# First layer's head of a hybrid decoder trunk: x in channel halves on a second queue, first weights in idle buffers, a written order for three engines

## The chip, the core and the metric

The kernel runs on one core of one Trainium2 chip. The metric is the device time of one execution in microseconds, the median of several runs; lower is better. Engines are called PE (TensorE), DVE (VectorE), ACT (ScalarE), POOL (GpSimd) and SP (SyncE, which only issues transfers here).

## What is computed

Two pre-norm decoder layers over 256 tokens with 1024 channels, batch 1. What matters here is the start of a layer:

```
h    = rms_norm(x, ln1_gain[l])            # over the 1024 channels
proj = h @ w_in[l]                         # 1024 -> several groups of columns
cos, sin = rope tables of positions        # three head groups use them
```

Columns of `proj` feed sparse attention (six heads), latent attention (five heads, low-rank queries and keys) and retention (five heads); their outputs go through `w_out`, and then comes a squared-ReLU MLP with `w_up` (1024 to 4096) and `w_down`. Everything is float32; the large products are made in three (or two) passes on a high and a low part of each operand.

## The kernel before

The 256 tokens are two tiles `t` of 128 rows. `xs` holds x with tokens on partitions; `xT` holds it transposed, channels on partitions, as a pair (high part, low part). Eight blocks `kt` of 128 channels make up the contraction.

**High and low parts.** `split` (L140 and L141) makes the pair: an ACT copy rounds the operand to the format of the fast product (`hi`), and a second engine, DVE unless told otherwise, subtracts it from the operand (`lo`). `mm3` (L146 to L148) makes three products of a pair with a pair. So each weight tile costs a transfer, an ACT copy, a DVE subtraction and then products on PE.

**The stream of weights.** `Stream` holds all weight tiles ("units") in the order of use. `get` loads up to LOAD_AHEAD units ahead and splits up to SPLIT_AHEAD ahead. Raw tiles come from a pool of five (`raw_tile`), split pairs from another pool of five (`hilo`); a transfer into a raw tile waits until the split that read it last is done. All transfers of units are issued by SP in the order of the list, one after the other. Eight semaphores go round among the transfers of the hardware queues, so a transfer also waits for the one eight places before it.

**The head.** Columns of `w_in` come in chunks: A (434 columns: gates and the latent vectors, four units of two channel blocks each, `raw_A`), then B2, B1, B3 (384 columns, four units each, `raw_B`), then rq, rk, rg, rv. For layer 0 the head loads constants `c0s` (identity matrix, frequencies), x and the gain, transposes x on PE (L486), multiplies by the gain on DVE (L493, `xg`), splits that into `xT`, and starts chunk A's products (48 of 128x434, `l_A`). Both tiles' halves are done by `norm_half`, four times. `rope_tables` computes sines and cosines of the positions: a chain of DVE operations on 128x96 values (`rt`), two sines on ACT, copies into `tab_c` and `tab_s`. `sum_sq` (L505) makes the sums of squares, from which the scale `rstd` follows; it is applied when a chunk leaves PSUM (L563). Eight products on zeros (`ps_idle`, L176) run on PE while nothing has landed. Two of chunk A's four low parts are made on POOL (START_POOL).

**The order** of the instructions on each engine comes from a scheduler in the tile framework that works with priorities (`PRIO`) and its own estimate of times; `issue_after` sets one instruction behind another. After chunk A the latent attention's small products (`ps_cT`, `ps_uq`, `ps_uk`, `ps_uv`) are mixed with B2 and B1. The compression weights (`raw_w`, eight transfers of 256 KB in rows of 512 bytes) come between B1 and B3 in the stream; their products are `ps_h`.

Of the kernel before, what the change touches and what calls it, by code (L numbers as in the profile page):

```python
# [48 lines left out]
START_POOL = (1, 2)  # L49
# [28 lines left out]
def tile_hybrid_trunk(  # L78
# [65 lines left out]
    def mm3(o, a, b, start, stop):  # L144

        nc.tensor.matmul(o, a[1], b[0], start=start, stop=False)  # L146
        nc.tensor.matmul(o, a[0], b[1], start=False, stop=False)  # L147
        nc.tensor.matmul(o, a[0], b[0], start=False, stop=stop)  # L148
# [16 lines left out]

    g8 = p2.tile([8, P], F32, name="g8", tag="h_sb", bufs=1)
    nc.sync.dma_start(c0s, c0)
    nc.sync.dma_start(xs[:, 0, 0:512], xv[:, 0, 0:512])
    nc.sync.dma_start(g8, ln1_gain[0].rearrange("(k p) -> k p", p=P))
    nc.sync.dma_start(xs[:, 0, 512:D], xv[:, 0, 512:D])  # L170
# [4 lines left out]
    for _ in range(WARM):  # L175
        nc.tensor.matmul(ps_idle[:, 0:P], idle, idle, start=True, stop=True)  # L176

    def late_start():
        nc.sync.dma_start(xs[:, 1, :], xv[:, 1, :])

    nc.gpsimd.dma_start(pos_i, positions.rearrange("o (t p) -> p (o t)", p=P))
# [18 lines left out]
    def rope_tables():  # L200
# [3 lines left out]
        nc.vector.tensor_copy(pos_f, pos_i)  # L204
# [3 lines left out]
        for t in range(2):  # L208
            nc.vector.tensor_scalar(ang[:, t], c0s[:, C_INV:C_INV + nf], pos_f[:, t:t + 1], None, op0=ALU.mult)

        def rounded(o, src, period):
            nc.vector.tensor_scalar(o, src, 1.0 / period, MAGIC, op0=ALU.mult, op1=ALU.add)
            nc.vector.tensor_scalar(o, o, MAGIC, None, op0=ALU.subtract)

        def less(o, k, part, src):
            nc.vector.scalar_tensor_tensor(o, in0=k, scalar=-part, in1=src, op0=ALU.mult, op1=ALU.add)
# [7 lines left out]
        nc.vector.tensor_scalar(u, k2, -small[2], None, op0=ALU.mult)  # L224
        less(u, k1, big[2], u)
        nc.vector.tensor_tensor(r, r, u, op=ALU.add)
        nc.vector.tensor_scalar(r, r, PI_LO, -PI_LO, op0=ALU.min, op1=ALU.max)
        nc.scalar.activation(s1, r, AF.Sin)
        nc.scalar.activation(s2, r, AF.Sin, scale=0.5)
        nc.vector.tensor_tensor(u, s2, s2, op=ALU.mult)  # L230
        nc.vector.tensor_scalar(u, u, -2.0, 1.0, op0=ALU.mult, op1=ALU.add)
        for off, sl, n in ((0, slice(0, 16, 2), 8), (16, slice(0, 16), 16), (48, slice(16, 48), 32)):
# [958 lines left out]
```

## Time and profile before

| | |
|---|---|
| time of three runs | 667.03, 668.58, 671.0 us; median 668.58 us |
| time of the profiled execution | 666.31 us |
| its span, first to last instruction | 664.5 us |
| PE busy | 641.7 us, 97% of the span |
| DVE, ACT, POOL busy | 456.0, 380.4, 75.6 us |
| mean granted TensorE clock | 0.991 of full speed |

The profile shows one execution. Its own time is 1.8 us over its span (start and end of the program), and 2.3 us below the median of the three runs. A row of a timeline gives start, duration, engine, line, operation, destination and sources; in brackets stand the engine's idle time ahead of it and what ended that. Consecutive instructions overlap a little, so a step costs less than its duration. SPq is SP issuing a transfer.

### The profile page before, as it was taken

The numbers are of one execution on the slowest core, as the hardware profiler recorded it, in microseconds if no ns is written. First come the engines' busy times: TensorE is split into PE (matmuls) and PEld (weight loads), VectorE is DVE, ScalarE is ACT, GpSimd is POOL, SyncE is SP. The second block draws the span as 40 slices with busy tenths as digits, with TensorE's granted clock in tenths as the row PEclk, the third lists the DMA queues.
The fourth block names the chain that finished last, engine by engine and source line by source line (L and its number), as shares of the span: only waits on it lengthen the run. The fifth ranks groups of instructions, "written<-read, shape, count | busy, mean of one in ns | idle before, by whom it ended". The sixth has DMA issues, their size and how long they took to land.

```text
span 664.5 us, 10416 instructions
## 1 busy us (share of the span) xinstructions
PE 641.7 (97%) x3619; PEld 549.9 (83%) x3619; DVE 456.0 (69%) x1059; ACT 380.4 (57%) x895; POOL 75.6 (11%) x128
## 2 busy tenths in 40 slices
PE   7998999999999999999999999999799999999995
PEld 6998997677888888888889999867588888888884
DVE  6756878767866666666676597877686666666663
ACT  5968776555554545454486787736384444444442
POOL 3520500210000000000033051130100000000000
PEclk7999999999999999999999999999999999999998
DMA  7897554043756565656548665423075665656521
GB/s 238 268 173 245 169 184 111 33 128 127 251 177 212 166 214 167 217 165 206 150 143 175 199 191 155 110 86 127 20 265 167 214 203 177 202 178 200 181 64 63
DMA packets 79797, 111.64 MB, mean 168 GB/s; under 512 B 9721, under 2 KB 67969, under 8 KB 79617
## 3 DMA queue, kind: packets, MB, share of 16 engines
q1 hardware_dynamic: 79136, 108.89, 54.0%
q0 software_dynamic: 608, 2.10, 0.9%
q8 instruction: 28, 0.46, 0.3%
q14 instruction: 25, 0.20, 0.1%
HBM read 109.92 MB, written 1.05 MB: 167 GB/s over the span
## 4 chain that ended last, share of the span: by engine, by line
PE 88%; DVE 5%; DMA 4%; ACT 2%; issue 1%; POOL 0%; POOLq 0%; SPq 0%; ACTq 0%; DVEq 0%
PE ps_up L1032 18%; PE ps_up L1033 9%; PE l_pd L146 9%; PE l_pd L148 9%; PE l_pd L147 9%; PE l_po L146 2%; PE l_po L148 2%; PE l_po L147 2%; DMA raw_rq<-in_w_in_dram 2%; PE l_oT L864 2%; PE l_B L146 1%; PE l_B L147 1%; PE l_B L148 1%; PE ps_pT L872 1%; PE ps_s L811 1%; DMA raw_B<-in_w_in_dram 1%
## 5 line engine op out<-in xcount | busy, mean ns | idle before, releaser
L1032 PE MATMUL ps_up<-xT,hi_wu 128*128 128x512 f32 x512 | 178.5, 393 | 0.5 <-DVE u_s L1044 0.5
L1033 PE MATMUL ps_up<-xT,lo_wu 128*128 128x256 f32 x512 | 140.6, 280 | 0.0
L141 DVE TENSOR_TENSOR lo_wd<-raw_wd,hi_wd 128x1024 fp32r<-128x1024 f32 x64 | 78.2, 1225 | 55.8 <-ACT hi_wd L140 55.4
L1032 PEld LDWEIGHTS ps_up<-xT,hi_wu 128*128 128x128 f32 x512 | 95.7, 188 | 22.0 <-DVE u_s L1044 1.1
L148 PE MATMUL l_pd<-hi_wd,u_h 128*128 128x512 f32 x256 | 100.6, 393 | 0.0
L146 PE MATMUL l_pd<-hi_wd,u_l 128*128 128x512 f32 x256 | 100.5, 394 | 0.0
L147 PE MATMUL l_pd<-lo_wd,u_h 128*128 128x512 f32 x256 | 99.7, 390 | 0.0
L1033 PEld LDWEIGHTS ps_up<-xT,lo_wu 128*128 128x128 f32 x512 | 96.0, 188 | 2.1
L140 ACT CAST hi_wu<-raw_wu 128x512 fp32r<-128x512 f32 x128 | 72.5, 618 | 35.3 <-issue 27.0
L141 DVE TENSOR_TENSOR lo_wu<-raw_wu,hi_wu 128x512 fp32r<-128x512 f32 x128 | 82.2, 686 | 14.5 <-ACT hi_wu L140 14.4
L140 ACT CAST hi_wd<-raw_wd 128x1024 fp32r<-128x1024 f32 x64 | 67.0, 1050 | 36.4 <-PE l_pd L148 22.3
L148 PEld LDWEIGHTS l_pd<-hi_wd,u_h 128*128 128x128 f32 x256 | 48.1, 188 | 11.2
L146 PEld LDWEIGHTS l_pd<-hi_wd,u_l 128*128 128x128 f32 x256 | 48.1, 188 | 10.2
L147 PEld LDWEIGHTS l_pd<-lo_wd,u_h 128*128 128x128 f32 x256 | 48.1, 188 | 9.6
L140 ACT CAST u_h<-u_u 128x512 fp32r<-128x512 f32 x32 | 19.8, 620 | 53.1 <-DVE u_u L1046 52.8
L1043 ACT COPY u_s<-ps_up 128x256 f32<-128x256 f32 x64 | 23.3, 368 | 36.8 <-PE ps_up L1033 36.8
L141 DVE TENSOR_TENSOR lo_B<-raw_B,hi_B 128x192 fp32r<-128x192 f32 (+1 forms) x80 | 28.6, 414 | 21.8 <-ACT hi_B L140 21.7
L1044 DVE TENSOR_TENSOR u_s<-ps_up,u_s 128x256 f32<-128x256 f32 x64 | 26.7, 421 | 23.0 <-ACT u_s L1043 23.0
L141 DVE TENSOR_TENSOR u_l<-u_u,u_h 128x512 fp32r<-128x512 f32 x32 | 22.1, 691 | 17.9 <-ACT u_h L140 17.9
L828 ACT ACTIVATE p_nsa<-p_nsa,nsa_m 128x256 f32<-128x256 f32 (+2 forms) x72 | 28.6, 400 | 8.0 <-DVE nsa_m L826 7.8
L147 PE MATMUL l_B<-lo_B,xT 128*128 128x384 f32 x96 | 32.9, 342 | 0.0
L140 ACT CAST hi_B<-raw_B 128x192 fp32r<-128x192 f32 (+1 forms) x80 | 25.1, 381 | 13.5 <-DMA raw_B<-in_w_in_dram 6.7
(320 smaller groups left out, 1246.1 us busy)
## 6 DMA issues: line engine op xcount, KB each, us to landing
raw_wu<-in_w_up_dram SPq DMA_DIRECT2D x64, 512.0 KB, 4.5
raw_wd<-in_w_down_dram SPq DMA_DIRECT2D x64, 512.0 KB, 4.2
raw_B<-in_w_in_dram SPq DMA_DIRECT2D x24, 384.0 KB, 3.8
raw_wo<-in_w_out_dram SPq DMA_DIRECT2D x10, 512.0 KB, 4.1
raw_A<-in_w_in_dram SPq DMA_DIRECT2D x8, 434.0 KB, 4.5
raw_wo<-in_w_out_dram SPq DMA_DIRECT2D x12, 256.0 KB, 4.2
raw_w<-in_cmp_w_k_dram SPq DMA_DIRECT2D x8, 256.0 KB, 6.1
raw_w<-in_cmp_w_v_dram SPq DMA_DIRECT2D x8, 256.0 KB, 5.7
```

What stands on the lines that cost most here:

```text
L140: a = nc.scalar.copy(out=hi, in_=src)
L141: b = eng.tensor_tensor(lo, src, hi.bitcast(F32), op=ALU.subtract)
L146: nc.tensor.matmul(o, a[1], b[0], start=start, stop=False)
L147: nc.tensor.matmul(o, a[0], b[1], start=False, stop=False)
L148: nc.tensor.matmul(o, a[0], b[0], start=False, stop=stop)
L811: nc.tensor.matmul(o, qT[g][:, r, t * P:(t + 1) * P], kT[i][:, g, a:b], start=i == 1, stop=i == 0)
L828: nc.scalar.activation(p[:, o:o + n], p[:, o:o + n], AF.Exp, scale=-1.0, bias=ms[:, r, b:b + 1], accum_out=ls[:, r, b:b + 1])
L864: nc.tensor.matmul(oT[gp, 0:384], kv_sb[kt][:, vi, gp], pTs[g][:, 0:384], start=i == 0, stop=False)
L1032: nc.tensor.matmul(ps[j], w[0][:, o:o + P], x2, start=i == 0 and k == 0, stop=False)
L1033: nc.tensor.matmul(ps[j][:, 0:S], w[1][:, o:o + P], x2[:, 0:S], start=False, stop=i == 1 and k == 3)
L1043: nc.scalar.copy(sj, ps[j][:, S:512])
L1044: nc.vector.tensor_tensor(sj, ps[j][:, 0:S], sj, op=ALU.add)
```

## The change

- x comes in four pieces (tile t, half h of the channels), issued by ACT on its own queue. First come the two first halves, with the gain between them. SP's queue starts with the constants, then the positions (before: issued by POOL), then chunk A's four units.
- Chunk A's raw weights go into the memory of `mixT`, which the mixers fill later. The five raw tiles are thereby free for B2's first unit, `uq`, `uk` and two more units of B2.
- A class `Line` sets each instruction of the head behind the one before it on the same engine: `vec` for DVE, `act_` for ACT, `ten` for PE. On DVE the whole first part of the rope tables comes first, then the gain, the splits of the first halves of x and of the first two units of A, then the rest of the tables. On ACT all sines come first. POOL makes no split any more.
- PE transposes the first halves of both tiles, makes another eight products on zeros (WARM_ON), then unit 0 of chunk A for both tiles; the second halves of x are transposed behind that.
- Splits of A come in pieces of 434 columns instead of 868. Chunk A accumulates in two other banks of PSUM (`att` in place of `acc`).
- The sines go straight to their tables with scale 1 or -1 (six ACT operations in place of one and six DVE copies); the cosine's last step writes the table.
- Small transfers of the mixers (`l_nrm`, `l_w2s`) move from SP to POOL, and the order of units puts B2's first unit ahead of the latent attention's.

```diff
-START_POOL = (1, 2)
+WARM_ON = 8
...
+    def x_part(t, h):
+        nc.scalar.dma_start(xs[:, t, h * 512:(h + 1) * 512], xv[:, t, h * 512:(h + 1) * 512])
...
     nc.sync.dma_start(c0s, c0)
-    nc.sync.dma_start(xs[:, 0, 0:512], xv[:, 0, 0:512])
-    nc.sync.dma_start(g8, ln1_gain[0].rearrange("(k p) -> k p", p=P))
-    nc.sync.dma_start(xs[:, 0, 512:D], xv[:, 0, 512:D])
+    x_part(0, 0)
+    nc.sync.dma_start(pos_i, positions.rearrange("o (t p) -> p (o t)", p=P))
+    nc.scalar.dma_start(g8, ln1_gain[0].rearrange("(k p) -> k p", p=P))
+    x_part(1, 0)
...
-    nc.gpsimd.dma_start(pos_i, positions.rearrange("o (t p) -> p (o t)", p=P))
...
-        nc.scalar.activation(s1, r, AF.Sin)
-        nc.scalar.activation(s2, r, AF.Sin, scale=0.5)
...
+        act_(lambda: nc.scalar.activation(s2, r, AF.Sin, scale=0.5))
+        groups = ((0, slice(0, 16, 2), 8), (16, slice(0, 16), 16), (48, slice(16, 48), 32))
+        for off, sl, n in groups:
             for half in range(2):
...
+                act_(lambda: nc.scalar.activation(tab_s[:, :, off + half * n:off + (half + 1) * n], r[:, :, sl], AF.Sin,
+                                                  scale=1.0 if half else -1.0))
...
         def load():
-            raw = raw_tile(name)
+            if home:
+                if home not in homes:
+                    homes[home] = p1.tile([P, 2, 1024], F32, name="raw_" + home, tag=home)
+                raw = homes[home][:, part]
+            else:
+                raw = raw_tile(name)
...
-                     nc.gpsimd if (l, name) == (0, "A") and i in START_POOL else nc.vector)
+                     home=f"mixT{i // 2}" if (l, name) == (0, "A") else None, part=i % 2)
...
+        add_chunk(l, "A")
+        add_chunk(l, "B2", 1)
         add_mla(l)
-        add_chunk(l, "B2")
+        add_chunk(l, "B2", 3, 1)
         add_cmp(l)
+        add_chunk(l, "B2", 4, 3)
...
+    class Line:
...
+        def __call__(self, f):
+            with tc.issue_after(self.last.ins) if self.last else nullcontext():
+                self.last = f()
...
+    def start_parts(hi, lo, src):
+        act_(lambda: nc.scalar.copy(out=hi, in_=src))
+        vec(lambda: nc.vector.tensor_tensor(lo, src, hi.bitcast(F32), op=ALU.subtract))
+        return act_.last, vec.last
...
-    for u in W.units[:W.index["x1"] + 1]:
+    for u in W.units[:4]:
         u[2] = u[0]()
         W.loaded += 1
+    x_part(0, 1)
+    x_part(1, 1)
...
+            W.hold((0, "B2", 0))
+            rope_finish = rope_tables(vec, act_)
+            ps = [start_transposes(0, 0)]
...
+            act_(lambda: sum_sq(0, 0, ss1))
+            ps.append(start_transposes(1, 0))
+            ten(lambda: warm(WARM_ON))
+            xg = [start_gain(t, 0, ps[t]) for t in range(2)]
+            start_x(0, 0, xg[0])
+            start_w(0, 0)
+            start_x(1, 0, xg[1])
+            start_w(0, 1)
+            start_w(1, 0)
+            start_w(1, 1)
+            rope_finish()
+            act_(lambda: sum_sq(1, 0, ss1))
...
+        def start_rest(ss1=ss1):
+
+            ps = [start_transposes(t, 1) for t in range(2)]
+            xg = [start_gain(t, 1, ps[t]) for t in range(2)]
+            for t in range(2):
+                start_x(t, 1, xg[t])
+            for i in (2, 3):
+                for j in range(2):
+                    start_w(i, j)
+            for t in range(2):
+                act_(lambda: sum_sq(t, 1, ss1))
+            factors()
+            W.load_to(LOAD_AHEAD)
+            W.release((act_.last, vec.last), SPLIT_AHEAD)
+            W.hold((0, "B2", 1))
```

The order of instructions that results, at two places. First ACT at the start of the program. Before (a DMA that an engine issues stands in its order too; `hi_A` and `raw_A` are the units of chunk A, `junk` is the sum of squares, `rt` the rope chain):

```order
L140 ACT_TABLE_LOAD
L140 CAST hi_A_202<-raw_A_103 128x868
L140 CAST xT<-xg 128x4x128 x2
L140 CAST hi_A_206<-raw_A_200 128x868
L140 CAST hi_A_212<-raw_A_210 128x868
L140 CAST xT<-xg 128x4x128
L140 CAST hi_A_218<-raw_A_216 128x868
L140 CAST xT<-xg 128x4x128
L505 ACTIVATE junk,l_ss_106<-xs 128x512 x4
```

and now (`raw_mixT` is chunk A's raw weights in their new place):

```order
L167 DMA xs<-in_x_dram 128x512 x3
L234 ACT_TABLE_LOAD
L234 ACTIVATE rt<-rt 128x96
L238 ACTIVATE tab_s<-rt 128x2x8 x2
L238 ACTIVATE tab_s<-rt 128x2x16 x2
L238 ACTIVATE tab_s<-rt 128x2x32 x2
L557 ACTIVATE junk,l_ss_111<-xs 128x512
L539 CAST xT<-xg 128x4x128
L539 CAST hi_A_168<-raw_mixT_103 128x434
L539 CAST xT<-xg 128x4x128
L539 CAST hi_A_168<-raw_mixT_103 128x434
L539 CAST hi_A_176<-raw_mixT_103 128x434 x2
```

Seven sines and one sum of squares now stand ahead of the first copy into `xT`. On DVE, likewise, all 16 operations of the rope chain (L209 to L233, the last of which writes the argument of the sines) stand ahead of the gain `gT`, which stood behind the seventh before.

Second, SP's transfers behind chunk A, up to the compression weights. Before (`l_pos_t` are 16 transfers of 8 KB, `c1s` the masks, 1056 KB):

```order
L371 DMA raw_uq_225<-in_mla_w_uq_dram 128x2x480
L402 DMA l_w2s<-in_cmp_w_k_dram 128x64
L404 DMA l_pos_t<-in_cmp_pos_k_dram 16x2x64 x2
L379 DMA raw_uk_227<-in_mla_w_ukv_dram 128x5x64 x2
L404 DMA l_pos_t<-in_cmp_pos_k_dram 16x2x64 x4
L323 DMA raw_B_0_230<-in_w_in_dram 128x2x384
L404 DMA l_pos_t<-in_cmp_pos_k_dram 16x2x64 x2
L323 DMA raw_B_1_232<-in_w_in_dram 128x2x384
L323 DMA raw_B_2_234<-in_w_in_dram 128x2x384
```

and now:

```order
L349 DMA raw_B_0_247<-in_w_in_dram 128x2x384
L397 DMA raw_uq_252<-in_mla_w_uq_dram 128x2x480
L405 DMA raw_uk_254<-in_mla_w_ukv_dram 128x5x64 x2
L349 DMA raw_B_1_257<-in_w_in_dram 128x2x384
L349 DMA raw_B_2_259<-in_w_in_dram 128x2x384
L430 DMA l_pos_t<-in_cmp_pos_k_dram 16x2x64 x8
L430 DMA l_pos_t<-in_cmp_pos_v_dram 16x2x64 x8
L480 DMA c1s<-c_dram 128x2113
L151 DMA l_gng<-in_ret_gn_gain_dram 128x320
L349 DMA raw_B_3_282<-in_w_in_dram 128x2x384
L349 DMA raw_B_0_301<-in_w_in_dram 128x2x384
L349 DMA raw_B_1_315<-in_w_in_dram 128x2x384
```

The five units behind chunk A now come in a row without a wait for a raw tile, and `c1s` stands ahead of B2's last unit, where it stood behind it.

## Rows read from the trace of the kernel before

**Rows 1.** The page, part 1: busy time and share of the span.
```profile
PE 641.7 (97%) x3619; PEld 549.9 (83%) x3619; DVE 456.0 (69%) x1059; ACT 380.4 (57%) x895; POOL 75.6 (11%) x128
```
**Rows 2.** Busy time by stretches, whole engines, with clock, DMA share and GB/s.
```profile
16.00:40.00 24.00, 24.00 (x133) 23.19 (x134) 17.18 (x58) 20.04 (x56) 10.41 (x22) 1.00 0.95 250
40.00:70.00 30.00, 27.38 (x221) 25.36 (x220) 20.19 (x67) 21.72 (x59) 6.06 (x16) 1.00 0.76 213
```
**Rows 3.** The same view in stretches of 1 us: the clock's fall and rise.
```profile
7.00:8.00 1.00, 0.00 (x0) 0.00 (x0) 1.00 (x3) 0.99 (x2) 0.00 (x0) 0.88 0.98 371
14.00:15.00 1.00, 1.00 (x4) 0.62 (x3) 1.00 (x1) 1.00 (x3) 1.00 (x1) 0.70 0.50 109
```
**Rows 4.** Timeline of PE in the head.
```profile
1.06 3.61 PE L176 MATMUL ps_idle<-idle 128*128 128x128 f32 x16 [1.06 <-DVE idle L173]
...
5.80 0.66 PE L486 MATMUL ps_xT<-c0s,xs 128*128 128x128 f32 x4 [0.27 <-DMA xs<-in_x_dram]
8.57 1.97 PE L486 MATMUL ps_xT<-c0s,xs 128*128 128x128 f32 x8 [2.12 <-DMA xs<-in_x_dram]
10.27 0.70 PE L146 MATMUL l_A<-hi_A,xT 128*128 128x434 f32 x1
...
15.95 0.47 PE L146 MATMUL l_A<-hi_A,xT 128*128 128x434 f32 x1 [0.91 <-DVE xT L141]
...
23.05 0.49 PE L592 MATMUL ps_cT<-c0s,l_a 128*128 128x128 f32 x3
```
**Rows 5.** Timeline of DVE in the head.
```profile
5.01 0.17 DVE L204 CAST pos_f<-pos_i 128x2 f32<-128x2 int32 x1 [4.01 <-DMA pos_i<-in_positions_dram]
...
6.73 0.21 DVE L212 TENSOR_SCALAR rt<-rt 128x96 f32<-128x96 f32 x1
...
7.57 0.69 DVE L493 TENSOR_TENSOR xg<-ps_xT,gT 128x512 f32<-128x512 f32 x1
...
21.61 1.02 DVE L141 TENSOR_TENSOR lo_B<-raw_B,hi_B 128x384 fp32r<-128x384 f32 x2
```
**Rows 6.** Timeline of ACT in the head.
```profile
7.83 1.14 ACT L140 CAST xT<-xg 128x512 fp32r<-128x512 f32 x2
...
14.43 0.62 ACT L505 ACTIVATE junk<-xs 128x512 f32<-128x512 f32 x1
...
19.67 0.27 ACT L229 ACTIVATE rt<-rt 128x96 f32<-128x96 f32 x1
...
20.56 0.91 ACT L140 CAST hi_B<-raw_B 128x384 fp32r<-128x384 f32 x2
```
**Rows 7.** Transfers of the first 60 us: count, KB each, median us to landing.
```profile
xs<-in_x_dram SPq DMA_DIRECT2D x2, 256.0 KB, 3.5
...
c0s<-c_dram SPq DMA_DIRECT2D x1, 88.0 KB, 2.0
...
pos_i<-in_positions_dram POOLq DMA_DIRECT2D x1, 1.0 KB, 3.7
```
**Rows 8.** Timeline of SP: when transfers are issued.
```profile
1.20 0.42 SPq L168 DMA_DIRECT2D xs<-in_x_dram  x1
...
29.20 3.85 SPq L416 DMA_DIRECT2D raw_w<-in_cmp_w_k_dram  x4
...
39.54 0.37 SPq L323 DMA_DIRECT2D raw_B<-in_w_in_dram  x1
```
**Rows 9.** Timeline of ACT around the first unit of B3.
```profile
45.73 1.12 ACT L140 CAST hi_B<-raw_B 128x192 fp32r<-128x192 f32 x4 [2.73 <-DMA raw_B<-in_w_in_dram]
```
**Rows 10.** What PE waited for between 40 and 70 us: us in total, times, longest.
```profile
PE l_rq L146 <- ACT l_kv L563: 1.3, 1, 1.3
PE ps_qkT L632 <- ACT l_qkT L633: 0.9, 2, 0.5
PE ps_h L731 <- ACT l_T L716: 0.3, 1, 0.3
```
**Rows 11.** The chain of waits, one piece of it.
```profile
54.46 6.51 DMA raw_rq<-in_w_in_dram
```

More of the change, by code (lines that the diff above doesn't have):

```diff
@@ L147, in mm3 @@
         nc.tensor.matmul(o, a[0], b[1], start=False, stop=False)
-        nc.tensor.matmul(o, a[0], b[0], start=False, stop=stop)
+        return nc.tensor.matmul(o, a[0], b[0], start=False, stop=stop)
     def bcast_row(t, row, n):
@@ L174, in tile_hybrid_trunk, with warm @@
     ps_idle = acc("ps_idle")
[L175 to L179, printed above, removed]
-    nc.gpsimd.dma_start(pos_i, positions.rearrange("o (t p) -> p (o t)", p=P))
+    def warm(n):
+        for _ in range(n):
+            last = nc.tensor.matmul(ps_idle[:, 0:P], idle, idle, start=True, stop=True)
+        return last
+    warm(WARM)
     ident = c0s[:, C_ID:C_ID + P]
@@ L286, in get, with load_to @@
             return u[3] if u[1] else u[2]
+        def load_to(self, n):
+            while self.loaded < n:
+                u = self.units[self.loaded]
+                u[2] = u[0]()
+                self.loaded += 1
         def hold(self, key):
@@ L549, in inproj @@
             n = CHUNKS[name][1]
-            ps = [acc(f"{L}{name}{t}") for t in range(2)]
+            if (l, name) == (0, "A"):
+                ps = [att(f"{L}{name}{t}", "MN"[t]) for t in range(2)]
+            else:
+                ps = [acc(f"{L}{name}{t}") for t in range(2)]
             for i, ks in enumerate(KSETS[n]):
-                w = W.get((l, name, i))
+                start = (l, name, i) == (0, "A", 0)
+                w = W.units[0][3] if start else W.get((l, name, i))
                 for t in range(2):
@@ L555, in inproj, with product @@
                     for j, kt in enumerate(ks):
-                        mm3(ps[t][:, 0:n], (xT[0][:, kt, tk], xT[1][:, kt, tk]),
-                            [z[:, j * n:(j + 1) * n] for z in w], start=kt == 0, stop=kt == 7)
+                        def product():
+                            return mm3(ps[t][:, 0:n], (xT[0][:, kt, tk], xT[1][:, kt, tk]),
+                                       [z[:, j * n:(j + 1) * n] for z in w], start=kt == 0, stop=kt == 7)
+                        if start:
+                            ten(product)
+                        else:
+                            product()
+                if start:
+                    start_rest()
             with prio(name):
                 for t in range(2):
-                    evac(t, ps[t][:, 0:n])
+                    last = evac(t, ps[t][:, 0:n])
+            return last
         def scaled(o, i, t):
-            nc.scalar.activation(o, i, AF.Copy, scale=rstd[:, t:t + 1])
+            return nc.scalar.activation(o, i, AF.Copy, scale=rstd[:, t:t + 1])
         a_sb = [None, None]
```

123 lines of the change are left out of this document (66 added, 57 removed).

## The prediction

> **What bounds the kernel now.** The page comes first: PE is busy for 641.7 of 664.5 us [rows 1], so a change can win only where PE waits or runs slowly. The stretches say where that is. From 16 to 40 us PE is never idle; from 40 to 70 us it is busy for 27.38 of 30 us, so 2.6 us are lost there [rows 2]. What is lost ahead of 16 us is read from PE's timeline: the first product of chunk A starts at 10.27, the fourteenth at 15.95, and the last of the 48 is over when `ps_cT` starts at 23.05 [rows 4]. The 35 products between 15.95 and 23.05 take 0.203 us each; the first 13 take 5.68 us where they would take 2.6 at that pace. The granted clock tells why: it is 0.88 on average between 7 and 8 us and 0.70 between 14 and 15 us, at half (1.2 GHz of 2.4) between the two [rows 3]. It fell while PE had nothing to do from 6.46 (5.80 + 0.66) to 8.57, waiting for the second tile of x, and came back some 5.8 us after PE had gone on [rows 3, 4].
>
> So the head holds 3.1 us of slow products and 10.3 us ahead of the first one, and the stretch from 40 to 70 us holds 2.6 us. There PE waits for ACT each time: 0.9 and 0.3 us for copies out of PSUM, 1.3 us for the evacuation ahead of chunk rq [rows 10]. ACT is late since it stood for 2.73 us, until 45.73, at the first unit of B3 [rows 9], which SP had issued at 39.54, behind the compression weights begun at 29.20 [rows 8]. The chain of waits shows the same for rq: a transfer of 6.51 us [rows 11].
>
> **The first product now.** x no longer decides it. Both engines' written orders begin with the rope chain, and that begins with the positions.
>
> The positions were issued on POOL and took 3.7 us to land; the only small transfer at the head of SP's queue, `c0s`, took 2.0 [rows 7]. They now stand second on SP, where an issue began at 1.20 [rows 8]. So they land at 3.2 to 4.9; I take 3.8, nearer to `c0s`, as it is the same queue, but with many pieces of four bytes. Before, DVE had them at 5.01 [rows 5].
>
> The rope chain is 16 operations on DVE. Eight of DVE's operations, seven of them of that chain, took from 5.01 to 6.73, 0.215 each [rows 5]; the second half waits for itself more often, so I take 3.7 us. It ends at 7.5. ACT then makes seven sines and one sum of squares. A sine of 96 columns takes 0.27, overlapping its neighbour, and most are smaller; I take 0.17 each, 1.2 in all, and 0.65 for the sum of squares with its read-out [rows 6]. So ACT copies the first piece of x from 9.4 to 9.95 (two of these took 1.14) [rows 6], DVE subtracts in 0.6 [rows 5], and the first product starts at 10.55: 0.3 us later than before.
>
> From there DVE and ACT alternate. The low part of unit 0's second piece is the fourth subtraction; with 0.6 for 512 columns and 0.52 for 434 (two of 384 took 1.02) [rows 5] it is there at 12.2. Eight of unit 0's products are still to do then (1.6 us), then eight transposes, which took 1.97 at half clock [rows 4], so 1.0, then 36 products at 0.203, 7.3 us. Chunk A ends at 12.2 + 1.6 + 1.0 + 7.3 = 22.1, against 23.05: **0.9 us won**, and with the positions at 3.2 or 4.9 it is 1.5 or -0.2. DVE's last low part of A is ready some 3 us ahead of the end, so the splits don't decide it. The price of the sines in front is thus paid back by the clock: no slow products.
>
> **What costs nothing here, and its cover.** The second halves of x, with all of x on ACT's queue: PE wants them behind unit 0, at 13.8; before, the last of x had landed by 8.57 [rows 4]. Chunk A's units 2 and 3: DVE wants them at about 16. The sums of squares and `rstd`: wanted when A leaves PSUM; ACT has them by about 19. POOL's seven small transfers: the first that is read is for the latent attention, behind A. The two low parts that POOL loses are in the DVE count above. The other four pieces of the rope tables fill DVE while PE works on unit 0. If one of these covers went, the price would be the lateness itself, on PE.
>
> **Behind chunk A.** The order on all engines is the same as before from B3 on, but for a few rows where layer 1 starts. Two things change up to there.
>
> The transfers. Five units follow chunk A without waiting for a raw tile, so what stands ahead of the compression weights is issued earlier. Its last unit's raw tile still comes free only when B2's last split is done, which I put at 29.4 (22.1, 36 products of 384 columns at about 0.18, as 434 take 0.203, and the split's 0.9), like now; but B1 lies in the queue earlier, so the compression weights run down earlier. B3's first unit is issued when B1's last split is done, about as now. What its landing gains lies between 0 and ACT's whole wait of 2.73; I take 2. ACT's lateness goes with it, and PE's waits for it, 1.2 us by rows plus some short ones; I count 1.2 won. SP issues B3's next units when the tile of the one before is free, so those too come earlier, and fewer bytes stand ahead of rq: of its 1.3 us I count 0.8. Together **2.0 us won**, with bounds of 0 and 2.6 [rows 2, 10].
>
> B1's last unit. Its split pair is that of `uq`, free after the last `ps_uq` product. Nine other products stood between that and its first use; now three do. A copy and a subtraction of 384 columns take 0.46 and 0.51 [rows 5, 6], three products of `ps_uk` about half of that: **0.3 us lost**, 0 to 0.6.
>
> The sum: 0.9 + 2.0 - 0.3 = 2.6 us. Against the profiled execution's own 666.31 us that is 663.7. The median of the three runs is 2.3 us higher than that execution, so as a median I expect 666.0.
>
> **Rivals.**
>
> *All of it comes.* The positions land like `c0s`, at 3.2, and all of PE's waits between 40 and 70 us go: 1.5 + 2.6 = 4.1 us, 664.5 as a median. For it: the same queue, and that all those waits hang on one late transfer. Against it: pieces of four bytes, and that rq's transfer waits for PE's own `ps_h`.
>
> *The waits behind stay.* The compression weights start no earlier than 29.2, and the queue is busy with them until B3's first unit: then only the head and B1's loss count, 0.9 - 0.3 = 0.6 us, 668.0. For it: the raw tile that they wait for comes free at the same time. Against it: only the first of them waits for that tile.
>
> *The clock falls in the wait.* PE transposes x of tile 0 right behind the first eight products on zeros, which end at 4.67 [rows 4], and then waits for tile 1's first half. Before, 604 KB stood up to the piece that PE had at 5.80 [rows 4]; now chunk A's first unit, 434 KB, runs beside it, at 371 GB/s [rows 3] up to 1.2 us more. So it comes between 5.8 and 7.0. The clock fell about 1.3 us after PE had gone idle at 6.46 [rows 3, 4], so from some 6.5 on this decides. Then the next eight products on zeros, 3.6 us at full clock [rows 4], stand ahead of chunk A at half clock; with the clock back after 5.8 us they end at about 13.9, and A ends at 13.9 + 48 x 0.203 + 1.0 = 24.6, 1.5 us later than before: 670.1. The Trainium skill speaks for this rival ("DMA: Bandwidth & Descriptors", section "Issuing engines are not separate DMA queues"): transfers of all engines run on the same 16 DMA engines and interleave, and a second issuing engine saves only the time of issue. By that rule tile 1's half would come at the late end. The trace of before has one hardware queue, so it can't tell.
>
> **How the numbers follow.** About 0.5% (3.3 us) is what a measurement of this kernel tells from no change. Forecast 0.50, its own range 664.9 to 667.4; all of it 0.28; waits stay 0.14; clock falls 0.08. Faster by over 0.5%: the second case and the upper part of the forecast, 0.38. Slower by over 0.5%: only if the clock's fall adds to the waits behind, 0.03. The rest, 0.59, is within it. The range that leaves 2 in 10 out reaches from a little beyond the second case to a little beyond the third, 663.2 to 669.2.
>
> **What would show it.** The rope chain starts on DVE between 3.2 and 4.9 and the first product near 10.5, with the clock at 1.00 from there. The eight transposes stand between unit 0 and unit 1, and `ps_cT` or B2 follows A at about 22. ACT's wait ahead of B3's first unit is under 1 us, and PE's waits between 40 and 70 us add up to less than 1. The prediction fails if the positions take 4 us or more on SP, if PE's clock is at half anywhere behind 8 us, or if PE finds a new wait at B2 or B1 of more than the 0.3 us.

## The result, and the profile after

The changed kernel took 673.79 us, median of 19 runs (670.34 to 676.23); the kernel before took 671.0 in 19 runs beside it. The ratio is 1.0054, with an interval from 1.0035 to 1.0072 (the two medians alone would give 1.0042): slower by half a per cent, where 666.0 was forecast. The profiled execution took 674.66 us, with a span of 672.5.

Page part 1 of the changed kernel, then its stretches (columns as in [rows 2]):

```profile
PE 647.0 (96%) x3635; PEld 553.5 (82%) x3635; DVE 455.2 (68%) x1058; ACT 381.2 (57%) x903; POOL 74.6 (11%) x135
```

```profile
16.00:40.00 24.00, 20.10 (x100) 18.41 (x99) 15.46 (x39) 18.29 (x50) 7.48 (x16) 0.93 0.72 207
40.00:70.00 30.00, 28.36 (x222) 26.47 (x220) 17.14 (x57) 21.59 (x57) 4.55 (x11) 1.00 0.77 195
```

Between 16 and 40 us PE was never idle before [rows 2]; now it is idle for 3.9 us there, and the clock is 0.93. Between 40 and 70 us its busy time rose by 1.0 us, half of the 2.0 that was looked for. The timeline of PE has the place, and ACT's what it waits for:

```profile
8.54 1.11 PE L529 MATMUL ps_xT<-c0s,xs 128*128 128x128 f32 x4 [3.08 <-DMA xs<-in_x_dram]
9.44 2.98 PE L182 MATMUL ps_idle<-idle 128*128 128x128 f32 x16
12.18 0.44 PE L146 MATMUL l_A<-hi_A,xT 128*128 128x434 f32 x1
...
23.03 0.52 PE L146 MATMUL l_B<-hi_B,xT 128*128 128x384 f32 x2
...
34.05 0.62 PE L146 MATMUL l_B<-hi_B,xT 128*128 128x384 f32 x2 [3.85 <-ACT hi_B L140]
```

```profile
8.27 0.28 ACT L234 ACTIVATE rt<-rt 128x96 f32<-128x96 f32 x1 [2.82 <-DVE rt L233]
...
9.82 0.60 ACT L539 CAST xT<-xg 128x512 fp32r<-128x512 f32 x1
...
33.48 0.93 ACT L140 CAST hi_B<-raw_B 128x384 fp32r<-128x384 f32 x2 [4.74 <-DMA raw_B<-in_w_in_dram]
```

Chunk A ends at 23.03, as before (23.05, [rows 4]). Eleven us later PE stands for 3.85 us at B2's last unit, since its raw weights land only at 33.5. SP's timeline says why:

```profile
14.94 5.66 SPq L430 DMA_DIRECT2D l_pos_t<-in_cmp_pos_k_dram  x8
20.64 4.65 SPq L430 DMA_DIRECT2D l_pos_t<-in_cmp_pos_v_dram  x8
25.33 0.42 SPq L480 DMA_DIRECT2D c1s<-c_dram  x1
25.80 0.43 SPq L151 DMA_DIRECT2D l_gng<-in_ret_gn_gain_dram  x1
26.35 2.72 SPq L349 DMA_DIRECT2D raw_B<-in_w_in_dram  x5
```

The load of that unit is the first of the five `raw_B` at 26.35. A raw tile was free for it at 22.7, when `uq` had been split on DVE:

```profile
21.34 1.35 DVE L415 SCALAR_TENSOR_TENSOR lo_uq<-raw_uq,l_nrm,hi_uq 128x480 fp32r<-128x480 f32 x2
```

Sixteen transfers of 8 KB, 10.3 us of SP together, `c1s` and `l_gng` stood in front. That is 0.64 us each on average, but an issue alone is shorter: by the median it takes 0.42 us, in the kernel before as in the changed one (the tile's issues of the first 60 us, before and after, with min/median/max ns):

```profile
L404 SPq DMA_DIRECT2D l_pos_t<-in_cmp_pos_k_dram x16: 311/420/626, 8.5 to 49.5; - x16
L430 SPq DMA_DIRECT2D l_pos_t<-in_cmp_pos_k_dram x16: 311/422/1106, 14.9 to 53.9; - x16
```

1.7 us of the rest is waiting. A transfer waits for the one eight places before it, and those were the loads of `uk` and of two units of B2 (what SP waited for between 14 and 26 us, with the us in total, the times and the longest):

```profile
SPq L430 <- DMA raw_B<-in_w_in_dram: 1.4, 2, 0.7
SPq L430 <- DMA raw_uk<-in_mla_w_ukv_dram: 0.3, 1, 0.3
```

The change's own order of units has a part in this: it writes the compression's transfers, `l_pos_t` among them, ahead of B2's last unit, where the kernel before wrote all of B2 first. How large that part is isn't shown. `c1s` and `l_gng` are written behind that unit and were issued ahead of it all the same, and in the kernel before too small transfers went out ahead of units that were written first. Writing the unit first again was not tried.

PE's hole then costs a second time, by stretches (same columns as above):

```profile
34.00:36.00 2.00, 1.95 (x8) 1.66 (x9) 1.97 (x6) 2.00 (x7) 0.00 (x0) 0.87 1.07 378
36.00:38.00 2.00, 2.00 (x7) 1.93 (x7) 2.00 (x8) 2.00 (x8) 0.00 (x0) 0.50 0.85 221
38.00:40.00 2.00, 2.00 (x10) 1.76 (x10) 1.54 (x6) 1.07 (x4) 0.00 (x0) 0.78 1.18 213
```

The clock fell to half (1.2 GHz of 2.4) soon after PE had stood, and PE worked on at half: 2.00 x 0.50 + 2.00 x 0.22 + 2.00 x 0.13 = 1.7 us lost. How late PE is from there on is seen where it begins two later chunks; the instructions of one tile on PE, with count, min/median/max ns and the first and last start in us, of the kernel before and then of the changed one:

```profile
L146 PE MATMUL l_rq<-hi_rq,xT x32: 308/308/417, 65.2 to 392.7; 128*128 128x320 f32 x32
L146 PE MATMUL l_po<-hi_wo,l_mixT x64: 387/394/503, 103.8 to 476.4; 128*128 128x512 f32 x64
```

```profile
L146 PE MATMUL l_rq<-hi_rq,xT x32: 305/309/416, 69.9 to 397.7; 128*128 128x320 f32 x32
L146 PE MATMUL l_po<-hi_wo,l_mixT x64: 388/394/503, 108.4 to 484.4; 128*128 128x512 f32 x64
```

At the first `l_rq` PE is 4.7 us late, and still 5.0 at the last one in layer 1: 3.85 + 1.7 + 0.3 (B1's last unit) less the waits won behind. The other 3 us of the 8 between the two profiled spans came between 397 and 484, where the clock fell in one profiled execution and not in the other:

```profile
470.00:480.00 10.00, 7.86 (x32) 4.30 (x32) 5.12 (x12) 2.13 (x5) 1.80 (x2) 0.66 0.00 0
```

Before, that stretch had 1.00. One profile of each kernel can't put this down to the change: the same stretch has 0.66 in before_two below, which has no part of the change, and it has 0.76 in pp_x2late and 1.00 in pos_pool, whose orders on PE are the same row for row. So a span was also split by its mean clock, for every run: span x (1 - clock) is what half clock cost. By medians the changed kernel lost 8.1 us to it and the kernel before 6.0 to 7.3 (four sets, measured beside the experiments below, with medians from 668.83 to 670.73); what is left, span x clock, is 664.2 against 660.8 to 662.3. So some 2 to 3 us of the loss are in waits, and one or two in the clock.

### The profile page after: what moved, and what is told of

Its sections match the earlier page's. It is cut to its first block, busy times and chain, and to the rows that moved or that the text cites. A ratio compares the mean times of both kernels' runs of the same rounds, so it can differ in the third digit from the quotient of the medians.

```text
span 672.5 us, 10458 instructions
## 1 busy us (share of the span) xinstructions
PE 647.0 (96%) x3635; PEld 553.5 (82%) x3635; DVE 455.2 (68%) x1058; ACT 381.2 (57%) x903; POOL 74.6 (11%) x135
## 4 chain that ended last, share of the span: by engine, by line
PE 87%; DMA 5%; DVE 3%; ACT 2%; issue 1%; SPq 0%; POOL 0%; POOLq 0%; ACTq 0%
PE ps_up L1130 18%; PE ps_up L1131 9%; PE l_pd L146 9%; PE l_pd L148 9%; PE l_pd L147 9%; PE l_po L146 2%; PE l_po L148 2%; PE l_po L147 2%; DMA raw_rq<-in_w_in_dram 2%; PE l_oT L962 2%; DMA raw_B<-in_w_in_dram 2%; PE l_B L146 2%; PE l_B L147 2%; PE l_B L148 2%; DMA raw_mixT<-in_w_in_dram 1%; PE ps_pT L970 1%
## 5 line engine op out<-in xcount | busy, mean ns | idle before, releaser
L146 PE MATMUL l_B<-hi_B,xT 128*128 128x384 f32 x96 | 32.2, 350 | 4.1 <-ACT hi_B L140 4.1
L141 DVE TENSOR_TENSOR u_l<-u_u,u_h 128x512 fp32r<-128x512 f32 x32 | 22.1, 690 | 17.9 <-ACT u_h L140 17.9
L147 PE MATMUL l_B<-lo_B,xT 128*128 128x384 f32 x96 | 33.5, 349 | 0.0
```

Source lines behind the costliest of these rows:

```text
L141: b = eng.tensor_tensor(lo, src, hi.bitcast(F32), op=ALU.subtract)
```

## Experiments

Theory A: the loss is what stands on SP ahead of B2's last unit (and of B1 behind it). Its rivals: the new head or its second queue costs it (B); it is only the clock's chance (C). "Before" in each diff is the changed kernel if nothing else is said. Ratios are to the kernel before, each with its interval.

### Four first cuts

**c1_behind.** `c1s` and `l_gng` behind the unit (`l_gng` in both layers):

```diff
+        with tc.issue_after(issued[l, "B2", 3].ins):
+            bcast_row(gng, ret_gn_gain[l].rearrange("h d -> (h d)"), 320)
...
-            W.add("c1", lambda: nc.sync.dma_start(c1s, c1) and None)
+            def load_c1():
+                with tc.issue_after(issued[0, "B2", 3].ins):
+                    nc.sync.dma_start(c1s, c1)
+            W.add("c1", load_c1)
```

> The changed kernel with one thing else: the loads of c1s and l_gng of the first layer may only be issued behind that of B2's last unit; the 16 small l_pos_t transfers still stand ahead of it. Theory A (the loss is B2's last unit landing late because of what stands ahead of it on SP): its load is issued at 25.3 us and not at 26.35, and no longer shares the engines with c1s' 1056 KB, lands near 29.3, is split by 30.3; the 3.85 us hole of TensorE at 30 us shrinks to 0.5 or less, the clock stays at full speed behind it, and of the 4.7 us that the changed kernel had lost at its first l_rq product some 4 come back: ratio to the kernel before 0.998 to 1.000. Theory B (the head, its second queue or the written order cost the time, and the hole only takes up slack): the hole closes and the time stays, ratio 1.003 to 1.007. Theory C (the loss is the clock's fall near 470 us in the one profiled execution, chance): ratio 1.004 to 1.007 too, with the hole closed and no fall near 470 us needed.

Measured: 672.53 us, 1.0044 (1.0024 to 1.0063). B2's hole closed, as all theories had it, but the time hardly moved. Timeline of ACT, then of PE:

```profile
29.91 0.93 ACT L140 CAST hi_B<-raw_B 128x384 fp32r<-128x384 f32 x2 [0.19 <-DMA raw_B<-in_w_in_dram]
...
33.55 2.13 ACT L140 CAST hi_B<-raw_B 128x192 fp32r<-128x192 f32 x8 [1.95 <-DMA raw_B<-in_w_in_dram]
```

```profile
36.20 0.44 PE L146 MATMUL l_B<-hi_B,xT 128*128 128x384 f32 x1 [1.12 <-ACT l_kc L664]
```

B2's last unit is now in time: it went out at 25.46, 0.9 us sooner, and took 4.4 us from issue to landing, where it took 7.1 with `c1s`' 1056 KB in front of it. The next one in the queue, B1's first, is late instead (`c1s` went out in front of it), ACT is late behind it, and PE waits at B1. In this execution A also ended 1.0 us later than in the changed kernel's. So theory A fails in its narrow form: not one unit is late but the queue.

**pos_pool.** The first layer's small transfers on POOL's queue:

```diff
-                    nc.sync.dma_start(pos_t[rep * 16:(rep + 1) * 16, z], pe[l].rearrange("(b a) d -> a b d", b=2))
+                    (nc.gpsimd if l == 0 else nc.sync).dma_start(pos_t[rep * 16:(rep + 1) * 16, z], pe[l].rearrange("(b a) d -> a b d", b=2))
```

> The changed kernel with the first layer's 16 small l_pos_t transfers on POOL's queue in place of SP's. Theory A: SP goes on to c1s near 15 us, B2's last unit is issued as soon as a raw buffer comes free (21.3 us, behind the split of B2's first unit), lands near 25, and TensorE finds no hole at B2; B1's units and the compression weights come some 5 us earlier too: ratio 0.996 to 0.999. Rival D (small transfers cost as much from POOL's queue, and share the engines with x and the A weights in the head): A ends 1 us or more later than 23.0, ratio 0.999 to 1.002. Theories B and C: 1.003 to 1.007.

Measured: 668.68 us, 0.9989 (0.9975 to 1.0004). In the traces 3 of PE's 3635 products stand elsewhere than in the changed kernel. The loss is gone; the first `l_rq` starts at 64.1. B and C can't give that.

**b20_in_wait.** B2's first unit split ahead of x's second halves:

```diff
             act_(lambda: sum_sq(1, 0, ss1))
+            W.load_to(5)
+            start_b2()
...
+            W.done = 5
             factors()
```

> The changed kernel with the split of B2's first unit moved into ScalarE's idle stretch ahead of x's second halves (13.6 to 16.0 us), so that its raw buffer comes free near 15.5 us and not 21.3. The 16 small transfers stay ahead of B2's last unit on SP, c1s and l_gng come behind it. Theory A: as with c1s held back, last unit issued near 25, landed near 29, hole 0.5 us or less, ratio 0.998 to 1.000; the two extra subtractions on VectorE (1.0 us) may put off x's second halves and A's end by up to 0.6. If A ends a microsecond or more later than 23.0, the written order of the head had no room: ratio 1.000 to 1.002. Theories B and C: 1.003 to 1.007.

Measured: 674.64 us, 1.0080 (1.0054 to 1.0107), worse than the change. The last unit went out at 25.79 and the hole at B2 closed, but A's second half came later (A ended at 26.38), the sums that hang on it too, and PE found another hole, 3.24 us, at `ps_uq`. The written order had no room.

**no_warm_on.** The eight products on zeros ahead of chunk A left out:

```diff
-            ten(lambda: warm(WARM_ON))
```

> The changed kernel without the eight warm products ahead of the first l_A product (nothing else changed; these products' results are not used). Theory H (they buy the clock): the first l_A product starts near 11.7 us in place of 12.18 but at half clock, as in the kernel before, full clock comes 3 us or more later, and A ends at 24 to 25.5 us in place of 23.03; a later end of A hides the late last unit of B2 in part, so the time grows less than A's end: ratio 1.005 to 1.009. Rival: they only stand in the way; A ends 0.5 us sooner, ratio 1.0045 to 1.005.

Measured: 673.46 us, 1.0058 (1.0039 to 1.0078). A began at 11.29 and ended at 24.68, 1.6 later than 23.03; the hole at B2 (1.95 us now) hid a part of that. It says nothing on the time; hence pp_warm0 below.

### The queue by itself

**pos_two, before_two.** 16 transfers merged into 4, in both layers; on the changed kernel, and on the kernel before:

```diff
-                for rep in range(8):
-                    nc.sync.dma_start(pos_t[rep * 16:(rep + 1) * 16, z], pe[l].rearrange("(b a) d -> a b d", b=2))
+                for b in range(2):
+                    nc.sync.dma_start(pos_t[:, z, b], pe[l][b * 16:(b + 1) * 16].unsqueeze(0).broadcast_to([8, 16, 64]))
```

> The changed kernel with the small l_pos_t loads of both layers merged: two transfers of 128 rows for each of k and v (the source's 16 rows read eight times by one transfer) in place of eight of 16 rows; on SP as before, same data. Theory A (what stands ahead of B2's last unit and of B1 on SP's queue is the loss, by its number of issues): SP is done with l_pos_t 7 us or more sooner, c1s goes out near 18, B2's last unit when its buffer is free at 21 to 22, TensorE finds no hole at B2; ratio 0.996 to 0.999, as with l_pos_t on POOL's queue (0.9989). If it is the bytes of small rows that cost and not the issues, the four take as long as the 16 and the ratio stays 1.003 to 1.007.

> The kernel before with the same merging of l_pos_t alone (no part of the change). It tells what the change's other parts are worth once SP's queue is free of the small issues. Theory A': the kernel before loses some of its own 2.6 us of TensorE waits between 40 and 70 us to the same queue, so it gains 1 to 2: ratio 0.997 to 0.9985; then pos_two below it shows the head's worth, and pos_two at it shows that the new head is worth nothing. Rival: its units and small transfers are interleaved on SP and nothing waits for them there: 0.999 to 1.001.

Measured: 673.92 us, 1.0060 (1.0034 to 1.0086), and 673.29 us, 1.0046 (1.0029 to 1.0063). Both missed, and neither tells of the queue: the scheduler had put some 200 of PE's 3635 products elsewhere (some 220 of 3619 in the second). In pos_two:

```profile
L146 PE MATMUL l_rq<-hi_rq,xT x32: 308/309/415, 63.6 to 398.3; 128*128 128x320 f32 x32
L146 PE MATMUL l_po<-hi_wo,l_mixT x64: 392/394/503, 106.1 to 484.9; 128*128 128x512 f32 x64
```

The first `l_rq` is the earliest of all runs, 6.3 us ahead of the changed kernel's; from there to the first `l_po` it takes 42.5 us in place of 38.5, as other work stands in between, and the clock falls once more in the wait behind. What that order costs in full was not tried.

**pos0_two.** The same for the first layer alone; PE, ACT and DVE have the order of the changed kernel row for row:

```diff
+                if l == 0:
+                    for b in range(2):
+                        nc.sync.dma_start(pos_t[:, z, b], pe[l][b * 16:(b + 1) * 16].unsqueeze(0).broadcast_to([8, 16, 64]))
-                for rep in range(8):
+                for rep in range(8 if l else 0):
```

> The changed kernel with the first layer's l_pos_t alone merged into four transfers of 128 rows on SP; the second layer keeps its 16. Unlike the run that merged both layers, the order on TensorE, ScalarE and VectorE is that of the changed kernel row for row; only SP's queue is shorter, by 12 issues. Theory A (the first layer's loss is what stands ahead of B2's last unit and B1 on SP, by its issues): no hole at B2, first l_rq product near 64 us, ratio 0.997 to 1.0005, as with l_pos_t on POOL's queue. Rival (what made the run with l_pos_t on POOL's queue good was a better head in it, and SP's issues matter little): ratio 1.002 to 1.006.

Measured: 669.32 us, 0.9992 (0.9967 to 1.0016). SP's timeline and the tile on PE:

```profile
14.62 1.86 SPq L431 DMA_DIRECT2D l_pos_t<-in_cmp_pos_k_dram  x2
16.52 1.24 SPq L431 DMA_DIRECT2D l_pos_t<-in_cmp_pos_v_dram  x2
17.81 0.45 SPq L483 DMA_DIRECT2D c1s<-c_dram  x1
18.30 0.43 SPq L151 DMA_DIRECT2D l_gng<-in_ret_gn_gain_dram  x1
23.49 4.24 SPq L349 DMA_DIRECT2D raw_B<-in_w_in_dram  x5
```

```profile
L146 PE MATMUL l_rq<-hi_rq,xT x32: 305/309/416, 64.9 to 392.8; 128*128 128x320 f32 x32
```

This is the cleanest pair. Twelve issues fewer on SP, 7.2 us less of it (10.3 to 3.1), the other engines' order unmoved. SP now waits for the raw tile and not the tile for SP, until `uq` has been split:

```profile
22.11 1.35 DVE L415 SCALAR_TENSOR_TENSOR lo_uq<-raw_uq,l_nrm,hi_uq 128x480 fp32r<-128x480 f32 x2
```

There is no hole between 16 and 40 us, and 5.0 us are back at `l_rq`, though A ended 0.8 us later than in the changed kernel's profile. Theory A holds, as a matter of the queue; the run takes away the issues and the waits between them together and doesn't part the two. The Trainium skill has the rule ("DMA: Bandwidth & Descriptors", section "Rules for kernel authors"): many small transfers should be merged into one. The trace agrees, but here the price is not the bytes' time on the DMA engines, which moved 16 GB/s between 20 and 24 us of the changed kernel (280 in pos0_two), but SP's: 0.64 us each with the waits, in front of loads that were wanted. The changed kernel in that stretch (columns as in [rows 2]):

```profile
20.00:24.00 4.00, 4.00 (x23) 3.83 (x22) 3.49 (x9) 4.00 (x10) 2.85 (x5) 1.00 0.08 16
```

**no_home.** A's raw weights back in the raw tiles:

```diff
-                     home=f"mixT{i // 2}" if (l, name) == (0, "A") else None, part=i % 2)
+                     home=None)
```

> One part of the change undone: A's raw weights back in the five raw tiles, all else as changed, the order on TensorE row for row the same. On SP all 16 l_pos_t transfers, c1s and l_gng then stand ahead of three of B2's units and not one. Theory A (the loss is what stands on SP ahead of B2's units while their buffers are taken): B2's second unit goes out near 26 us and lands near 30 to 31 where TensorE wants it at 25.7, the hole moves forward and grows to 5 us or more, ratio 1.007 to 1.011. Rival (the idle homes are what makes the late load, since they let B2's first unit, uq and uk fill the raw tiles early): with A's raw tiles freed one by one the hole closes, ratio 0.998 to 1.002.

Measured: 675.79 us, 1.0077 (1.0052 to 1.0101), with the order on PE unchanged:

```profile
31.22 1.01 PE L146 MATMUL l_B<-hi_B,xT 128*128 128x384 f32 x2 [3.96 <-ACT hi_B L140]
```

The hole came forward to B2's second unit, as theory A had it, though it stayed at 3.96 us where 5 or more was put. So the idle homes are not the fault: without them fewer units go out ahead of the small transfers, and the hole is still there. Whether they help can't be told by the time (1.0077 against 1.0054, with intervals that overlap).

### The head

With the queue relieved, A's end is no longer hidden. These runs ask why the head wins nothing.

**pp_warm0, pp_x2late**, on pos_pool: without the eight warm products; and with x's second halves on SP, behind A's second unit:

```diff
-            ten(lambda: warm(WARM_ON))
```

```diff
-    for u in W.units[:4]:
...
-    x_part(0, 1)
-    x_part(1, 1)
+    W.load_to(2)
+    x_part(0, 1, nc.sync)
+    x_part(1, 1, nc.sync)
+    W.load_to(4)
```

> The changed kernel with l_pos_t of the first layer on POOL's queue (so that no hole at B2 hides the head's end), and without the eight warm products ahead of the first l_A product. Theory H (the warm products buy the clock): A's products run at half clock into 15 us or later, A ends at 23.3 to 25 us against 22.5 with them, ratio 1.000 to 1.003. Rival (they only stand in the way): first product 0.3 us sooner, A ends at 22.5 or before, ratio 0.997 to 0.999.

> The changed kernel with l_pos_t of the first layer on POOL's queue, and x's second halves issued from SP behind the first two weight units of A in place of ACT's queue right behind the first halves. Theory X (x's first half of tile 1 is late because the second halves and the weights share the engines with it): it lands at 6.5 to 7.2 us in place of 7.6 to 8.5, the warm products start that much sooner, the first l_A product stands near 10.9 (bound then by the sines and the x copies on ACT) and A ends 0.3 to 0.6 us sooner; ratio 0.996 to 0.999. Rival (it is late for SP's weights alone): it lands where it did, and nothing changes: 0.998 to 1.000.

Measured: 669.36 us, 1.0001 (0.9982 to 1.0020), and 669.57 us, 1.0002 (0.9982 to 1.0021), against 0.9989: neither is told from it. In their profiles A ended at 24.29 and 24.23 (pos_pool 22.46). For the warm products theory H holds in the trace: without them A takes 13.4 us from its first product, with them 11.1, and 13.4 against 10.85 in no_warm_on and the changed kernel. Theory X fell: tile 1's half landed at 8.6, no sooner.

**t0_x1sp**, on pos0_two: that half from SP right behind `c0s`, the positions on ACT's queue:

```diff
-    nc.sync.dma_start(pos_i, positions.rearrange("o (t p) -> p (o t)", p=P))
+    x_part(1, 0, nc.sync)
+    nc.scalar.dma_start(pos_i, positions.rearrange("o (t p) -> p (o t)", p=P))
...
-    x_part(1, 0)
```

> The changed kernel with the first layer's l_pos_t merged, and tile 1's first half of x issued from SP right behind c0s, with the positions and the gain going out from ACT's queue behind x's first part. Theory X' (it was late because it stood third on ACT's queue, behind the gain's eight rows, and was issued 0.6 us later than it could be): it lands at 5.5 to 6.8 us in place of 7.6 to 8.9, the warm products follow at once, full clock comes 2 us sooner, the first l_A product stands near 11.0 (bound by the sines and x copies on ACT), A ends near 22.0: ratio 0.4 to 0.8 us (0.001) below the run with l_pos_t merged alone. Rival (the engines are shared with the weights from 2 us on, whatever the queue): it lands at 7.5 or later, and nothing is gained.

**t0_rl**, on pos0_two: the rope chain behind the first splits; **t0_x1sp_rl**: both:

```diff
-            rope_finish = rope_tables(vec, act_)
...
             start_w(1, 1)
-            rope_finish()
+            rope_tables(vec, act_)()
```

> The changed kernel with the first layer's l_pos_t merged, and the rope chain and the sines written behind the splits of A's first two units in place of ahead of all else on VectorE and ScalarE. Theory R (with x's halves early enough the positions' chain of 3.9 us and the sines stand in front of the first x copy): x's first copy runs as soon as the tile is scaled, near 6.5, the first l_A product is bound by the landing of A's first unit (9.4) and of x's second tile (8.5), so it stands at 10.2 to 11.2 with the warm products behind x's second tile; A ends 0.5 to 1.5 sooner than 23.0; ratio 0.001 to 0.002 below the run with l_pos_t merged alone. Rival (x's second tile and the warm products behind it bound the start): first l_A product at 11.4 or later, nothing gained.

> All three: l_pos_t of the first layer merged, tile 1's first half of x from SP ahead of the weights, rope chain and sines behind the first splits. If both theories of the head hold the first l_A product stands near 9.5 (A's first unit lands at 9.4), A ends at 20.5 to 21.5 in place of 23.0, and half of that is lost again where B2's units wait for their raw buffers; ratio 0.995 to 0.998. If only one of them holds it equals that run.

Measured: 669.17 us, 1.0001 (0.9981 to 1.0020); 670.90 us, 1.0019 (0.9999 to 1.0040); 673.26 us, 1.0055 (1.0034 to 1.0077). PE's timeline in t0_x1sp, then in t0_x1sp_rl:

```profile
5.83 0.81 PE L532 MATMUL ps_xT<-c0s,xs 128*128 128x128 f32 x4
6.47 1.95 PE L182 MATMUL ps_idle<-idle 128*128 128x128 f32 x16
12.27 0.43 PE L146 MATMUL l_A<-hi_A,xT 128*128 128x434 f32 x1 [3.85 <-DVE xT L543]
```

```profile
9.91 0.47 PE L146 MATMUL l_A<-hi_A,xT 128*128 128x434 f32 x1 [1.59 <-ACT hi_A L542]
...
20.44 1.09 PE L146 MATMUL l_A<-hi_A,xT 128*128 128x434 f32 x2 [3.65 <-ACT hi_A L542]
```

From SP the half is there at 5.8: its place in the queues made it late (theory X'). The run moves it ahead of A's weights, to another engine and to an issue 0.6 us earlier, all at once, and doesn't part these. But then the positions came at 5.51 and the rope chain stood in the way, PE waited longer, 3.85 us, and A ended at 25.05, where 22.0 was put. In t0_rl the first product came at 12.50, since x's tile 1 landed at 8.3 and the warm products stood behind it, as the rival had it. With both, A began at 9.91, and the chain stood in the way of x's second halves: 3.65 us, the clock fell, A ended at 28.07, where 20.5 to 21.5 was put. None of the three gave the gain in time that was put.

**t0_x1sp_prope**: as t0_x1sp, with the chain on POOL, sines behind the first splits:

```diff
-            vec(lambda: nc.vector.scalar_tensor_tensor(o, in0=k, scalar=-part, in1=src, op0=ALU.mult, op1=ALU.add))
+            pol(lambda: nc.gpsimd.tensor_scalar(s1, k, -part, None, op0=ALU.mult))
+            pol(lambda: nc.gpsimd.tensor_tensor(o, s1, src, op=ALU.add))
...
             start_w(1, 1)
-            rope_finish()
             act_(lambda: sum_sq(1, 0, ss1))
+            rope_sines()
```

> The changed kernel with l_pos_t of the first layer merged, tile 1's first half of x from SP ahead of the weights, and the rope chain on POOL (each fused multiply and add as two instructions; the sines behind the first splits on ScalarE, the cosines' part behind A's last splits on VectorE). The two runs of the head before it each left one chain in the way: with the chain in front the first l_A product stood at 12.3, with the chain behind the first splits A started at 9.9 and then lost 3.65 us and the clock at x's second halves. Theory (these two places are all that keeps the head from paying): first l_A product at 9.9 to 10.2, no wait above 0.6 us in A, A ends at 20.8 to 22.0 in place of 23.0 to 23.8, ratio 0.996 to 0.998. Rival (POOL's instructions slow VectorE's, or A's later units land too late): A ends at 22.5 or later, 0.998 to 1.001.

Measured: 670.95 us, 0.9999 (0.9976 to 1.0023). PE's timeline, then ACT's:

```profile
9.19 0.47 PE L146 MATMUL l_A<-hi_A,xT 128*128 128x434 f32 x1 [0.90 <-ACT hi_A L545]
...
18.78 0.82 PE L146 MATMUL l_A<-hi_A,xT 128*128 128x434 f32 x2 [2.43 <-ACT hi_A L545]
```

```profile
16.22 0.28 ACT L238 ACTIVATE rt<-rt 128x96 f32<-128x96 f32 x1 [1.70 <-POOL rt L235]
```

A began 3.0 us sooner than in the changed kernel and ended at 25.63: POOL took 10.4 us for the chain, the sines came at 16.22, and ACT's copies of x's second halves queued behind them. The theory fell (A was to end at 20.8 to 22.0): the two places were not all; ACT's fixed order is a third. What a head without any of the three would win was not tried.

## Why the prediction was wrong

**The step that failed** is in "Behind chunk A": the raw tile that "still comes free only when B2's last split is done, which I put at 29.4", reckoned from PE's pace alone. The split was over at 35.0, as its weights landed at 33.5, and the compression weights, which take that tile, went out at 35.08 and not near 29.20 [rows 8]. With the queue relieved (pos0_two) they go out at 30.99, with A's end 1.7 us behind the 22.1 that was put: the pace was right, and what stood in SP's queue was left out. The order of SP was at hand; the sixteen rows were read as an order and not as 10.3 us. The kernel before gives a part of the price in one row of its SP timeline:

```profile
18.53 2.75 SPq L404 DMA_DIRECT2D l_pos_t<-in_cmp_pos_v_dram  x6
```

That is 0.46 each, so 7.3 us for sixteen and an issue of the unit at 23 or later, with `c1s` ahead of it. The other 3 us are waits for landings and a few slow issues, which that row doesn't have. There the small transfers stood between the loads, as A's raw tiles came free one by one; no rival had them as a block. So the 2.0 us "won behind" were right in kind, too large, and hidden by the hole. With the queue relieved (pos0_two) PE is busy for 28.32 of 30 us in [rows 2]'s second stretch, 0.9 more than before; with the 0.26 that B1's last unit cost (put at 0.3) that is 1.2 won where 2.0 was put, inside the bounds of 0 to 2.6. Of the prediction's own signs of failing, two came: a new wait at B2, and the clock at half behind 8 us.

**The head: 0.9 put, nothing measured.** The positions were on DVE at 4.36 (3.8 put, bounds 3.2 to 4.9), the chain took 3.9 (3.7; it has 15 operations, not the 16 that were counted), the first copy of x stood at 9.82 (9.4): each term a little small. The first product came at 12.18, not 10.55. Some 0.7 of that is those terms, as no_warm_on, with the first copy at 9.82 too and no warm products, began A at 11.29; the rest is that x's tile 1 landed at 8.5, outside the 5.8 to 7.0 that were allowed, and the warm products stood behind it. That is the third rival's condition, with its 0.08 far too low; it was to cost 1.5 us. Its price was off the other way. The clock in the changed kernel's profile (columns as in [rows 2]):

```profile
8.00:9.00 1.00, 0.46 (x2) 0.47 (x3) 0.94 (x3) 0.73 (x6) 0.00 (x0) 0.59 0.94 336
11.00:12.00 1.00, 1.00 (x8) 1.00 (x8) 1.00 (x3) 0.90 (x3) 0.00 (x0) 0.71 1.06 364
12.00:13.00 1.00, 1.00 (x8) 0.97 (x8) 1.00 (x3) 1.00 (x3) 0.00 (x0) 1.00 1.07 376
```

It was back at full by 12, some 3 us after PE had gone on at 8.54, where 5.8 was put. The "3.6 us at full clock" of eight products on zeros was misread: the same products take 1.95 us at a granted 1.00 in t0_x1sp's row above, and the 3.6 is the pace of the transposes at half clock (16 rows in 3.61, 8 in 1.97, [rows 4]). From the first product A took 10.85 us, put at 11.55. Of the 3.1 us that the prediction calls slow products, 0.91 was PE waiting for DVE, in the row at 15.95 of [rows 4]. Over the profiles of kernels with this head and warm products unchanged (the changed kernel, c1_behind, pos_pool, pos0_two) A ends at 23.03, 24.03, 22.46 and 23.81, and takes 10.85 to 11.55 us, so the head's worth is -1.0 to +0.6. The trace agrees with the rule of the Trainium skill that stood beside that rival ("DMA: Bandwidth & Descriptors", section "Issuing engines are not separate DMA queues"): what several engines issue shares the same DMA engines. Between 3 and 8 us SP's queue moved 0.58 MB and ACT's 0.46, and tile 1's half came late. What the runs add is that it comes at 5.8 when it stands ahead of A's weights on SP's queue, against 7.6 to 8.9 from ACT's.

**The sum.** Put were -0.9 (head), -2.0 (waits behind) and +0.3 (B1's last unit). In the profiles, up to the first `l_rq`, it was 0.0 for the head, +3.85 for the hole, +1.7 for the half clock behind it, +0.3 for B1's last unit, and what is left of the 4.7 us by which that row is late, -1.1, for the waits behind, as the busy time of that stretch has it (1.0, or 1.2 without B1's last unit). By the ratio the loss is 3.6 us of 671.0, by the medians 2.8: single executions differ by where the clock falls later, which no step of the prediction could know. Why it falls near 470 us in one execution and not in the next is open.

No version beat both kernels: pos_pool and pos0_two take back the change's loss, and neither can be told from the kernel before.

## What to carry to other kernels

When loads are made free of a buffer's wait, look at what then stands in the queue as a block: count every issue by its duration in a row, small transfers above all, and what each waits for, up to the first load that an engine wants. Here the small transfers were written ahead of the unit, and the scheduler put two more transfers, written later, in front of it; read the queue's order and put a time on each row. In a head with one fixed order, moving one chain out of the way shows the next: price all of them before moving one.

## What the runs showed of the hardware

Issuing a transfer of 8 KB kept SP 0.42 us by the median in both kernels (0.46 from one to the next in the row of the kernel before above); in the changed kernel's block it was 0.64 on average, with the waits for transfers eight places earlier. Merged into four transfers of 32 KB in pos0_two, they took 3.1 us. The same x half landed at 5.8 us from second place on SP's queue, ahead of A's weights, and at 7.6 to 8.9 from third on ACT's. The rope chain took 3.9 us on DVE in 15 instructions and 10.4 on POOL (20 instructions there, as each of five fused multiply and adds is two). The clock fell between 470 and 480 us in the profile of pp_x2late (0.76 on average) and not in that of pos_pool (1.00), with the same order on PE.
